# Keeping the traced order on VectorE and ScalarE from the big sets on, and asking sooner for w_down's operands and the last group's weights

## The chip, the cores and the metric

The kernel runs on one core of a Trainium2 chip. The metric is the device time of one execution in microseconds (us), taken as the median of several runs. TensorE is called PE in the profile, VectorE DVE, ScalarE ACT, GpSimd POOL and SyncE SP; SPq, ACTq and POOLq are the DMA queues that these engines issue into.

## The reference, cut to what matters

One transformer block with 512 tokens, width 2048 and a feed-forward width of 5632, all in float32. The mixing half (a latent-attention branch and a gated delta branch) is not touched by the change. What is touched is the second half and the final norm:

```
h = _rmsnorm(x, norm_ffn[l]) * (1.0 + sc_f) + sh_f
gate, up = jnp.split(h @ w_gate_up[l], 2, axis=-1)
x = x + gt_f * ((jax.nn.silu(gate) * up) @ w_down[l])
...
return _rmsnorm(x, final_norm)
```

## The kernel before

**Precision.** Every float32 operand of a matmul is split into two parts: `hi`, a cast on ScalarE to a rounded float32 format, and `lo`, the rest, subtracted on VectorE. A product is then three matmuls: hi with hi, hi with lo, lo with hi. In the trace a weight's halves are `hi` and `lo`, an operand's halves `xh`/`xl` (or `h2h`/`h2l`, `ah`/`al`), and the last group's weights `wl`. `hilo` (lines 238 to 247) makes an operand's two halves: lines 242 (ScalarE) and 243 (VectorE). A weight's halves are made at lines 1718 and 1721 (Strassen sets) or 266 and 267 (plain sets).

**Strassen sets.** `strassen` (line 1673) computes a product of 2 by 2 blocks with seven products, in 16 units. Units 0 to 7 work on four products (`m1`, `m6`, `m7`, `m5`; 24 matmuls a unit), units 8 to 15 on three (`m2`, `m4`, `m3`; 18 matmuls). A unit has a load (`start`, three DMAs of 256 KB on SP's queue), a split (`sums` on VectorE at line 1698, then a cast and a subtraction for each of two weight tiles), its matmuls, and sometimes a step ahead of them (`pre`) or behind them (`post`). In what follows a set's units are called u0 to u15.

**Order of the sets.** B1 to B10 are the big sets, `big(s)`, for w_gate_up (gate and up, then Silu and product in `finish`). Four plain sets dn0 to dn3 (`dn(36, n)`) follow for one group of w_down's rows, then two Strassen sets D0 and D1 (`strassen_down(0, n)`), four more plain sets dn4 to dn7 (`dn(40, n)`), the Strassen sets D2 and D3 (`strassen_down(1, n)`), and the last group (`last_down`): two `last_set`s and eight `token_unit`s, in the trace the matmuls with output `dnt`. A plain set has two units; its four PSUM banks are emptied by four ScalarE activations (tile `y`, line 2066), each followed by an accumulating DMA on POOL's queue. Between the plain sets dn1 and dn2 stand `turned_a` units: four short transposes, whose result is split into `ah` and `al`.

**Operands of the Strassen sets of w_down.** `sums_down(ks)` (line 1952) makes the operands for D0 and D1 (ks=0) or D2 and D3 (ks=1), in four parts q0 to q3; q is used by units 2q, 2q+1 and again 8+2q, 9+2q. A part reads four tiles of 256 KB back from `f_dram` (`a11`, `a21`, `a22`, `a12`, in the trace all named `a`), takes four sums on VectorE (line 1983) and makes seven pairs of halves (lines 242 and 243): 11 operations on VectorE and 7 on ScalarE. `free(q)` says when a part may start, by how many of the earlier operands are `gone`. A part that is not ready when a unit needs it is forced: `ready` (lines 1793 and 1835) steps the generator to the end of that part ahead of the unit's matmuls. While one part is computed, the loads of the next are fetched, one between two steps.

**Chains and the driver.** Generators such as `sums_down` are chains: the driver (line 49) steps each of them once for every 12 matmuls that it emits, and a `yield n` waits n such steps. The driver also loads units ahead: `drv.ahead` says how many units may be loaded beyond the two that are split. It is 4 (`LOADS`), and `pre` of a Strassen set's u0 sets it to 2.

**Order on the engines.** `Ordered` (line 144) wraps an engine: every instruction issued through it keeps its place in the traced order. In the kernel before TensorE, GpSimd and SyncE are wrapped, so the profile gives line 155 for all that they do; VectorE and ScalarE are not, and the scheduler places their instructions as it sees fit, but for those wrapped in `behind` (line 205): the sums of the weights and of the operands on VectorE.

**Last group.** `gated_weights` multiplies the last group's weights with the gate, splits them and writes them to `l_dram` during the big sets. `last_weights(n)` loads eight of these tiles (`wl`, 256 KB each) on SP's queue; n=0, 1, 2 at units 11, 13 and 15 of D3, n=3 ahead of the second `last_set`. `last_rows`, ahead of the first `last_set`, loads four rows of the final norm on the same queue. Each of the eight `token_unit`s (t, n), with n=2 and 3 in turn, is 12 matmuls.

Of the kernel before, what the change touches and what calls it, by code (L numbers as in the profile page):

```python
# [34 lines left out]
class Unit:  # L35


    def __init__(self, load=None, split=None, mms=None, pre=None, post=None, weight=1, alone=False, late=False):
        self.load = load
        self.split = split  # L40
        self.mms = mms
        self.pre = pre
        self.post = post
        self.weight = weight
        self.alone = alone
        self.late = late
# [97 lines left out]
class Ordered:  # L144


    def __init__(self, tc, engine):
        self.tc = tc
        self.engine = engine

    def __getattr__(self, name):
        f = getattr(self.engine, name)

        def call(*args, **kwargs):
            return self.tc.keep_in_program_order(f(*args, **kwargs))  # L155

        return call


class Core:  # L160
    def __init__(self, tc, pinned):
        nc = tc.nc
        for e in ("tensor", "vector", "scalar", "gpsimd", "sync"):
            setattr(self, e, Ordered(tc, getattr(nc, e)) if e in pinned else getattr(nc, e))

# [4 lines left out]
def block_kernel(ctx: ExitStack, tc: tile.TileContext, a: dict, out):  # L172
    nc = Core(tc, PINNED)
    drv = Driver()
# [28 lines left out]
        nc.gpsimd.dma_start(dst, src)  # L203

    def behind(ins):
        return tc.keep_in_program_order(ins)

    mm = nc.tensor.matmul

# [340 lines left out]
    def logits_done(first):  # L550
        def done(ps):
            for j, q in enumerate(ps):
# [6 lines left out]
                        ks=[(k, 1) for k in range(KT)])  # L559
# [900 lines left out]
    def with_pre(units, fn):  # L1460
        u = units[0]
        p0 = u.pre

        def pre():
            fn()
            if p0 is not None:
                p0()
        u.pre = pre
        return units
# [203 lines left out]
    def strassen(w, g, u, par, operand, ready, second_read, finish, freed, extra=None):  # L1673
# [53 lines left out]
        def pre(i):  # L1727
            ready(i % 8 // 2)
            if i == 0:
                drv.ahead = 2  # L1730
                for c, *_ in FIRST4:
                    ps[c] = [PS(c) for _ in range(2)]
            if i == 8 and "act" in chains:
                drv.finish(chains["act"])
# [154 lines left out]
    def gated_weights():  # L1889

        for n in range(4):
            row = gate_row(n)
            for k in range(4):
                w = S("wg")
                side(w[:], w_dn[(LAST + k) * P:(LAST + k + 1) * P, 512 * n:512 * n + 512])
                yield 4
                behind(nc.vector.tensor_tensor(w[:], w[:], row[:], ALU.mult))
                for i, v in enumerate(hilo(w[:], "wg")):
                    side(l_dram[n, k, i], v[:].bitcast(F32))
                w = v = None  # L1900
                yield 4
# [50 lines left out]
    def sums_down(ks):  # L1952

        ahead = []

        def free(q):
            return q < 4 and gone[ks] >= min(q + 2, 4) and (q < 3 or plain_sets[0] > 4 * ks + 3)

        def fetch_a(q):
            v = {}  # L1960
            for name, i, h in (("a11", 8 * ks + q, 0), ("a21", 8 * ks + q, 1), ("a22", 8 * ks + 4 + q, 1), ("a12", 8 * ks + 4 + q, 0)):
                v[name] = S(name)
                load(v[name][:], f_dram[i, h])
                yield 2
            ahead.append(v)

        for q in range(4):
            if not ahead:
                yield from until(lambda: free(q))
                yield from fetch_a(q)  # L1970
                yield 5
            v = ahead.pop(0)
            more = free(q + 1)
            if more:
                fetching = fetch_a(q + 1)
            v["x7"] = S("x7")
            d = {}
            for c, dst, x, y, op in (("m7", "x7", "a11", "a21", ALU.subtract), ("m1", "a11", None, None, None),
                                     ("m5", "a21", "a22", "a21", ALU.subtract), ("m4", "a22", None, None, None),
                                     ("m6", "a11", "a11", "a21", ALU.add), ("m2", "a12", None, None, None),  # L1980
                                     ("m3", "a12", "a11", "a12", ALU.subtract)):
                if op is not None:
                    behind(nc.vector.tensor_tensor(v[dst][:], v[x][:], v[y][:], op))
                d[c] = hilo(v[dst][:], "x")
                if op is None:
                    if more and next(fetching, None) is None:
                        more = False
                    yield
            v = None
            if more:  # L1990
                yield from fetching
            down[ks][q] = d
            made[ks] = q + 1
            yield
# [80 lines left out]
    xc = []  # L2075

    def ffn():
        def gu0():
            us, st = [], {}

            def done(ps):
                done_ = gu_done(0, ps)
                for j in range(4):
                    for h in range(2):
                        done_(j, h)

            for h in range(2):
                half = fm_set("gu0", gu_loads(0), 512, KT, lambda k, h=h: half_k(h2T[h][k // 2], k), done if h else None, st=st,
                              cols=slice(256 * h, 256 * h + 256), alone=True)
                for i, u in enumerate(half):  # L2090
                    def ahead(h=h, k=min(2 * i + 4, KT)):
                        while h2n[h] < k:
                            drv.step(h2c[h])
                    with_pre([u], ahead)
                us.append(half)

            def start():
                for j in range(KT):
                    mixT[j] = None
                start_h2(1)()  # L2100
            with_pre(us[0], start)
            return us[0] + us[1]
# [12 lines left out]
        def last_weights(n):  # L2115

            for k in range(4):
                wl[n, k] = S("wl", F32R), S("wl", F32R)
                for i in range(2):
                    load(wl[n, k][i][:].bitcast(F32), l_dram[n, k, i])  # L2120
# [34 lines left out]
        def last_down():  # L2155
            for i, u in enumerate(strassen_down(1, 1, turned_x2)):
                if 6 <= i < 14:
                    with_pre([u], lambda i=i: x2_back(i - 6))
                if i >= 12:
                    with_pre([u], lambda i=i: reload_a(LAST + i - 12))  # L2160
                if i in (11, 13, 15):
                    with_pre([u], lambda i=i: last_weights((i - 11) // 2))
                yield u
            for n in range(2):
                us = last_set(n)
                if n == 0:
                    with_pre(us, last_rows)
                else:
                    with_pre(us, lambda: last_weights(3))
                yield from us  # L2170
            for t in range(NT):
                for n in (2, 3):
                    yield token_unit(t, n)
# [54 lines left out]
        def scaled(t, y):  # L2228
            for i in range(4):
# [4 lines left out]
                    nc.vector.tensor_scalar(v, v, y[:], None, op0=ALU.mult)  # L2234
                (nc.scalar.dma_start if i % 2 else load)(out[tok(t), 512 * i:512 * i + 512], v)

        yield from gu0()
        yield from with_pre(gu_both(1), lambda: xc.append(drv.add(combine())))
        assert known == {4, 5}
        side(g_dram.rearrange("(k p) -> p k", p=P), gt_ffn[:])  # L2240
        euvw.append(wides.tile([P, 4, 512], F32, tag="wide", name="euvw"))
        drv.add(gated_weights())
        for s in range(1, 11):
            for i, u in enumerate(big(s)):
                if (s, i) == (10, 10):
                    with_pre([u], lambda: maker.__setitem__(0, drv.add(sums_down(0))))
                yield u

# [1 line left out]
            drv.ahead = LOADS  # L2250
        for n in range(4):
            for k, u in enumerate(dn(36, n)):
                yield with_pre([u], more)[0]
                if n in (1, 2):
                    yield Unit(mms=turned_a(2 * n + k - 2), pre=lambda: drv.finish(chains["act"]))
        for n in range(2):
            for i, u in enumerate(strassen_down(0, n)):
                if (n, i) == (1, 10):
                    def start():
                        for k in range(40, 44):  # L2260
                            reload_a(k)
                        maker[1] = drv.add(sums_down(1))
                    with_pre([u], start)
                yield u
        for n in range(4):
            for u in dn(40, n):
                yield with_pre([u], more)[0]
        yield from strassen_down(1, 0)
        yield from last_down()

# [59 lines left out]
```

## Time and profile before

| What | us |
|---|---|
| median of 3 runs | 2822.74 |
| lowest and highest of the runs | 2819.11, 2823.09 |
| the profiled execution | 2822.31 |
| its span, first to last instruction | 2820.5 |
| PE busy in the span | 2737.4 |
| DVE busy | 2012.8 |
| ACT busy | 1136.7 |
| POOL busy | 245.8 |

The profiled execution is 0.43 us under the median; 1.8 us of its time lie outside the span. A times row in the views of the trace starts with a window (from and to, in us from the span's start), its length, and each engine's busy time with the number of its instructions, then the clock granted to TensorE as a share of full speed, the mean share of time in which the 16 DMA engines were busy, and GB/s. A row of a timeline starts with the start and the duration in us; the brackets hold the idle time before the instruction and what ended it. A group's `x4` means four instructions in a row.

### The profile page before, as it was taken

The numbers are of one execution on the slowest core, as the hardware profiler recorded it, in microseconds if no ns is written. First come the engines' busy times: TensorE is split into PE (matmuls) and PEld (weight loads), VectorE is DVE, ScalarE is ACT, GpSimd is POOL, SyncE is SP. The second block draws the span as 40 slices with busy tenths as digits, with TensorE's granted clock in tenths as the row PEclk, the third lists the DMA queues.
The fourth block names the chain that finished last, engine by engine and source line by source line (L and its number), as shares of the span: only waits on it lengthen the run. The fifth ranks groups of instructions, "written<-read, shape, count | busy, mean of one in ns | idle before, by whom it ended". The sixth has DMA issues, their size and how long they took to land. (4 is left out here: it accounts for less than half of the span.)

```text
span 2820.5 us, 37178 instructions
## 1 busy us (share of the span) xinstructions
PE 2737.4 (97%) x13478; PEld 2282.4 (81%) x13478; DVE 2012.8 (71%) x3114; ACT 1136.7 (40%) x1593; POOL 245.8 (9%) x324
## 2 busy tenths in 40 slices
PE   9999999999999999999999999999999997997987
PEld 7888788888888888888997888888888885785775
DVE  8784657676867456883678888777778858767754
ACT  3443333443344332232554444444444444344332
POOL 0000011002100000000001011000000020111033
PEclk9999999999999999999999999999999998998998
DMA  9896556546755468894656667656666686687697
GB/s 353 297 353 203 157 168 185 180 146 184 210 148 179 145 213 277 283 310 138 188 168 211 233 226 239 213 202 199 206 209 214 212 216 187 225 258 182 164 300 214
DMA packets 319969, 606.00 MB, mean 215 GB/s; under 512 B 42948, under 2 KB 79972, under 8 KB 319656
## 3 DMA queue, kind: packets, MB, share of 16 engines
q1 hardware_dynamic: 255544, 482.06, 52.9%
q0 software_dynamic: 27744, 63.23, 8.5%
q10 hardware_dynamic: 36496, 58.34, 5.7%
q8 instruction: 105, 1.72, 0.2%
q14 instruction: 80, 0.66, 0.1%
HBM read 505.97 MB, written 97.53 MB: 214 GB/s over the span
## 5 line engine op out<-in xcount | busy, mean ns | idle before, releaser
L267 DVE TENSOR_TENSOR lo<-raw,hi 128x1024 fp32r<-128x1024 f32 (+1 forms) x274 | 336.8, 1230 | 314.7 <-ACT hi L266 301.0
L266 ACT CAST hi<-raw 128x1024 fp32r<-128x1024 f32 (+1 forms) x274 | 285.1, 1042 | 676.4 <-DMA raw<-in_w_in_dram 133.8
L1718 ACT CAST hi<-raws 128x1024 fp32r<-128x1024 f32 (+1 forms) x336 | 302.1, 908 | 553.7 <-DVE raws L1698 268.0
L1721 DVE TENSOR_TENSOR lo<-raws,hi 128x1024 fp32r<-128x1024 f32 (+1 forms) x336 | 350.4, 1043 | 194.5 <-ACT hi L1718 192.9
L438 DVE CUSTOM_DVE_ANT_0 rawm<-rawm,cbc 128x1024 f32<-128x1024 f32 x192 | 233.8, 1236 | 10.8 <-DMA rawm<-in_w_mod_dram 10.6
L155 PE MATMUL m<-hi,xh 128*128 128x512 f32 x448 | 183.6, 410 | 29.6 <-ACT xh L242 26.8
L155 PE MATMUL m<-lo,xh 128*128 128x512 f32 x448 | 182.2, 407 | 10.1 <-DVE lo L1721 9.9
L155 PE MATMUL m<-hi,h2h 128*128 128x512 f32 x480 | 190.5, 397 | 0.0
L155 PE MATMUL m<-lo,h2h 128*128 128x512 f32 x480 | 187.4, 390 | 1.7 <-DVE lo L1721 1.6
L155 PE MATMUL m<-hi,xl 128*128 128x512 f32 x448 | 182.4, 407 | 5.4 <-DVE xl L243 5.3
L155 PE MATMUL m<-hi,h2l 128*128 128x512 f32 x480 | 187.2, 390 | 0.0
L1698 DVE TENSOR_TENSOR sums<-raws,raws 128x1024 f32<-128x1024 f32 x112 | 136.3, 1218 | 30.2 <-DMA raws<-in_w_down_dram 17.6
L1721 DVE TENSOR_TENSOR lo<-sums,hi 128x1024 fp32r<-128x1024 f32 x112 | 136.3, 1217 | 22.0 <-ACT hi L1718 21.9
L1718 ACT CAST hi<-sums 128x1024 fp32r<-128x1024 f32 x112 | 117.4, 1048 | 51.5 <-PE m L155 51.4
L155 PEld LDWEIGHTS m<-hi,xh 128*128 128x128 f32 x448 | 88.7, 198 | 51.4 <-ACT xh L242 30.2
L155 PEld LDWEIGHTS m<-lo,xh 128*128 128x128 f32 x448 | 88.9, 198 | 32.5 <-DVE lo L1721 13.9
L155 PE MATMUL wo<-mh,hi 128*128 128x512 f32 (+1 forms) x320 | 111.2, 347 | 0.0
L155 PE MATMUL wo<-mh,lo 128*128 128x512 f32 (+1 forms) x320 | 111.0, 347 | 0.0
L155 PE MATMUL wo<-ml,hi 128*128 128x512 f32 (+1 forms) x320 | 110.9, 347 | 0.0
L155 PEld LDWEIGHTS m<-hi,xl 128*128 128x128 f32 x448 | 88.0, 197 | 27.6 <-DVE xl L243 9.6
L155 PEld LDWEIGHTS m<-lo,h2h 128*128 128x128 f32 x480 | 90.3, 188 | 21.2 <-DVE lo L1721 3.6
L155 PEld LDWEIGHTS m<-hi,h2l 128*128 128x128 f32 x480 | 90.1, 188 | 19.2
(521 smaller groups left out, 6896.2 us busy)
## 6 DMA issues: line engine op xcount, KB each, us to landing
raws<-in_w_gate_up_dram SPq DMA_DIRECT2D x400, 256.0 KB, 3.6
rawm<-in_w_mod_dram SPq DMA_DIRECT2D x192, 512.0 KB, 5.5
raw<-in_w_in_dram SPq DMA_DIRECT2D x144, 512.0 KB, 4.6
raws<-in_w_down_dram SPq DMA_DIRECT2D x160, 256.0 KB, 5.1
s_dram<-raws ACTq DMA_DIRECT2D x112, 256.0 KB, 2.2
raws<-s_dram SPq DMA_DIRECT2D x112, 256.0 KB, 3.7
raw<-in_w_o_dram SPq DMA_DIRECT2D x40, 512.0 KB, 4.3
rawa<-in_w_in_dram SPq DMA_DIRECT2D x32, 512.0 KB, 4.1
```

Source lines behind the costliest of these rows:

```text
L155: return self.tc.keep_in_program_order(f(*args, **kwargs))
L266: nc.scalar.copy(hi[:], raw[:])
L267: (lo_eng or nc.vector).tensor_tensor(lo[:], raw[:], hi[:].bitcast(F32), ALU.subtract)
L438: r = nc.vector.tensor_tensor_reduce(raw, raw, c, 1.0, 0.0, ALU.mult, ALU.add, parts[:, k, half:half + 1])
L1698: add = lambda o, x, y: behind(nc.vector.tensor_tensor(o, x, y, ALU.add))
L1718: nc.scalar.copy(hi[:], src)
L1721: nc.vector.tensor_tensor(lo[:], src, hi[:].bitcast(F32), ALU.subtract)
```

## The change

Three things are edited.

**Order.** `Ordered` gets a switch `on`. All five engines are wrapped now, VectorE and ScalarE with the switch off; it is turned on for both just before `gated_weights` is added, which happens while the last units ahead of B1 are fetched. From then on both engines keep the traced order. `behind` does nothing more once the switch is on.

**w_down's operands.** `sums_down(0)` starts at unit 8 of B10 (before: 10), `sums_down(1)` at unit 8 of D1 (before: 10), with the reload of `ah` and `al` for dn4 to dn7 moved from unit 10 to unit 13. `free` lets parts start after 0, 2, 3 and 4 of `gone` (before: 2, 3, 4, 4). `fetch_a` yields once, with no number, after each of its four loads (before: `yield 2`), and `yield 3` (before: 5) follows the fourth. `drv.ahead` is set to 2 at unit 3 of the second plain gate-and-up set and in the last two of each group of four plain sets, no longer in `pre` of a Strassen set.

**Last group's weights.** `last_weights(0..2)` move one unit earlier, to units 10, 12 and 14 of D3; `last_weights(3)` moves from the second `last_set` to the first, ahead of `last_rows`.

```diff
 class Ordered:
-    def __init__(self, tc, engine):
+    def __init__(self, tc, engine, on=True):
...
         def call(*args, **kwargs):
-            return self.tc.keep_in_program_order(f(*args, **kwargs))
+            ins = f(*args, **kwargs)
+            return self.tc.keep_in_program_order(ins) if self.on else ins
...
-            setattr(self, e, Ordered(tc, getattr(nc, e)) if e in pinned else getattr(nc, e))
+            setattr(self, e, Ordered(tc, getattr(nc, e), e in pinned))
...
     def behind(ins):
-        return tc.keep_in_program_order(ins)
+        return ins if nc.vector.on else tc.keep_in_program_order(ins)
...
             if i == 0:
-                drv.ahead = 2
...
         def free(q):
-            return q < 4 and gone[ks] >= min(q + 2, 4) and (q < 3 or plain_sets[0] > 4 * ks + 3)
+            return q < 4 and gone[ks] >= (0, 2, 3, 4)[q] and (q < 3 or plain_sets[0] > 4 * ks + 3)
...
                 load(v[name][:], f_dram[i, h])
-                yield 2
+                yield
             ahead.append(v)
...
                 yield from fetch_a(q)
-                yield 5
+                yield 3
...
-                if i in (11, 13, 15):
-                    with_pre([u], lambda i=i: last_weights((i - 11) // 2))
+                if i in (10, 12, 14):
+                    with_pre([u], lambda i=i: last_weights((i - 10) // 2))
...
                 if n == 0:
-                    with_pre(us, last_rows)
-                else:
-                    with_pre(us, lambda: last_weights(3))
+                    with_pre(us, lambda: (last_weights(3), last_rows()))
...
+        def few():
+            drv.ahead = 2
+
         yield from gu0()
-        yield from with_pre(gu_both(1), lambda: xc.append(drv.add(combine())))
+        us = with_pre(gu_both(1), lambda: xc.append(drv.add(combine())))
+        with_pre([us[3]], few)
+        yield from us
...
+        nc.vector.on = nc.scalar.on = True
         drv.add(gated_weights())
         for s in range(1, 11):
             for i, u in enumerate(big(s)):
-                if (s, i) == (10, 10):
+                if (s, i) == (10, 8):
                     with_pre([u], lambda: maker.__setitem__(0, drv.add(sums_down(0))))
...
-                yield with_pre([u], more)[0]
+                yield with_pre([u], more if n < 2 else few)[0]
...
-                if (n, i) == (1, 10):
+                if (n, i) == (1, 13):
+                    with_pre([u], lambda: [reload_a(k) for k in range(40, 44)])
+                if (n, i) == (1, 8):
                     def start():
-                        for k in range(40, 44):
-                            reload_a(k)
                         maker[1] = drv.add(sums_down(1))
...
-                yield with_pre([u], more)[0]
+                yield with_pre([u], more if n < 2 else few)[0]
```

The loop in `sums_down` that fetches the next part between two steps is unchanged. It reads:

```python
if more and next(fetching, None) is None:
    more = False
```

More of the change, by code (lines that the diff above doesn't have):

```diff
@@ L144 @@
 class Ordered:
-    def __init__(self, tc, engine):
+    def __init__(self, tc, engine, on=True):
         self.tc = tc
         self.engine = engine
+        self.on = on
     def __getattr__(self, name):
```

## The prediction

> **What bounds the kernel now.** First the page: how much of the span TensorE (PE) is busy, and which of its matmuls wait.
>
> ```profile
> span 2820.5 us, 37178 instructions
> ...
> PE 2737.4 (97%) x13478; PEld 2282.4 (81%) x13478; DVE 2012.8 (71%) x3114; ACT 1136.7 (40%) x1593; POOL 245.8 (9%) x324
> ...
> L155 PE MATMUL m<-hi,xh 128*128 128x512 f32 x448 | 183.6, 410 | 29.6 <-ACT xh L242 26.8
> ```
>
> PE is the bound, and no edit takes a matmul away (its instructions and their order are the same in both programs). So only PE's 83 us of idleness, and the slower clock that follows an idle stretch, can be won or added to. The last row says where: matmuls of w_down's Strassen sets wait for the operand's cast. Next, busy time by stage: B2 to dn0, dn0 to dn3, D0, D1, dn4 to dn7, D2, D3.
>
> ```profile
> 1500.00:2300.00 800.00, 798.32 (x3582) 659.22 (x3581) 629.22 (x736) 356.77 (x439) 48.99 (x86) 1.00 0.65 217
> 2279.40:2324.90 45.50, 45.50 (x210) 37.64 (x209) 24.23 (x31) 20.86 (x31) 19.26 (x20) 1.00 0.95 229
> 2324.90:2427.00 102.10, 85.85 (x337) 67.98 (x336) 79.95 (x100) 45.80 (x60) 6.63 (x7) 0.90 0.61 178
> 2427.00:2507.30 80.30, 77.33 (x337) 62.69 (x336) 61.74 (x74) 30.01 (x34) 10.10 (x19) 1.00 0.79 259
> 2507.30:2550.90 43.60, 43.60 (x194) 36.09 (x193) 25.43 (x31) 21.73 (x30) 18.81 (x21) 1.00 1.06 258
> 2550.90:2655.70 104.80, 86.07 (x338) 67.61 (x337) 76.92 (x97) 43.16 (x57) 6.00 (x7) 0.89 0.58 165
> 2655.70:2754.60 98.90, 88.67 (x401) 71.17 (x400) 61.61 (x74) 34.05 (x46) 29.17 (x43) 0.97 0.95 279
> ```
>
> The plain sets and the big sets have no gap worth the name and run at full clock: there is nothing to win there, only something to lose. A Strassen set's 8 x 24 + 8 x 18 = 336 matmuls, 0.227 us apart, need 76.2 us. D0 takes 102.1 and D2 104.8: 25.9 and 28.6 us too many, at a clock of 0.90. D1 is 4.1 over; D3's 98.9 hold 64 short transposes besides. Third, what PE waits for from dn0 on:
>
> ```profile
> PE m L155 <- ACT xh L242: 26.8, 7, 6.6
> PE m L155 <- DVE lo L1721: 9.9, 7, 3.3
> PE dnt L155 <- DMA wl<-l_dram: 6.0, 5, 1.5
> PE m L155 <- DVE xl L243: 5.3, 6, 1.7
> PE m L155 <- ACT y L2066: 2.7, 1, 2.7
> ```
>
> The operand parts (xh, xl) carry 32 of these 51 us. Where they bite, unit by unit (u0, u2, u4, u6 of D0; u1, u2, u4, u6 of D2; ideal 24 x 0.227 = 5.44 us each):
>
> ```profile
> 2324.87:2334.79 9.92, 7.19 (x25) 5.42 (x24) 8.25 (x10) 6.49 (x9) 4.06 (x4) 0.84 0.74 200
> 2340.39:2354.15 13.76, 7.66 (x26) 5.80 (x24) 11.80 (x15) 5.73 (x8) 0.00 (x0) 0.75 0.79 242
> 2359.59:2373.20 13.61, 9.07 (x25) 6.29 (x24) 11.86 (x16) 4.99 (x7) 0.58 (x1) 0.75 0.48 158
> 2378.64:2388.90 10.26, 7.38 (x25) 5.32 (x24) 8.48 (x13) 4.46 (x7) 0.57 (x1) 0.83 0.70 217
> ```
> ```profile
> 2556.29:2568.46 12.17, 5.60 (x25) 4.32 (x23) 7.25 (x9) 4.23 (x6) 0.00 (x0) 0.95 0.86 241
> 2568.46:2582.71 14.25, 9.50 (x24) 6.59 (x25) 12.16 (x16) 4.83 (x7) 0.00 (x0) 0.57 0.37 112
> 2588.15:2601.83 13.68, 9.14 (x26) 6.31 (x24) 11.87 (x16) 4.99 (x7) 0.58 (x1) 0.75 0.51 156
> 2607.27:2617.57 10.30, 7.43 (x25) 5.36 (x24) 8.49 (x13) 4.46 (x7) 0.57 (x1) 0.83 0.69 217
> ```
>
> Over 5.44 they are: D0 4.5, 8.3, 8.2, 4.8; D2 6.7, 8.8, 8.2, 4.9. Part q1 is needed at u2, q2 at u4, q3 at u6. A part of each excess is gap and a part clock (0.57 to 0.95 in these rows).
>
> **The change part by part.** Working base: the profiled execution, 2822.31 us (0.43 under the median), of which 2820.5 are span.
>
> *The end of dn3 and D0's u0.* Operand casts run on ScalarE (ACT) ahead of dn3's evictions, because the part's loads stood on SP behind nine weight loads that took 32.61 us to issue:
>
> ```profile
> 2292.73 32.61 SPq L155 DMA_DIRECT2D raws<-in_w_down_dram  x9
> ```
> ```profile
> 2329.75 2.41 ACT L2066 ACTIVATE y<-dn,gt_ffn 128x512 f32<-128x512 f32 x4
> ```
> ```profile
> 2330.48 0.50 PE L155 MATMUL m<-hi,xh 128*128 128x512 f32 x1 [2.73 <-ACT y L2066]
> ```
>
> The changed program asks for q0 in B10 and q1 from B10's u15 on, with fewer weights loaded ahead: q0 is computed in B10, q1 in dn1 and dn2, and y stands first on ACT. u0's 4.5 and u2's 8.3 us go.
>
> *q2 and q3 of D0.* `fetch_a` now yields None, and the loop takes a None for the end of the fetch. So only `a11` is fetched ahead, then dropped: six loads more (1.5 MB; hidden, DMA share 0.61 in D0), and each part begins its four loads anew once the part before is done. In the traced order q2 falls into D0's u1 to u3 and q3 is still due when u6 needs it, so its whole chain is forced ahead of u6. How long a chain takes is seen in dn2, from the first sum to the last subtraction:
>
> ```profile
> 2304.57 0.68 DVE L1983 TENSOR_TENSOR x<-a,a 128x512 f32<-128x512 f32 x1
> ...
> 2314.40 0.69 DVE L243 TENSOR_TENSOR xl<-a,xh 128x512 fp32r<-128x512 f32 x1 [0.69 <-ACT xh L242]
> ```
>
> That is 10.5 us. In a fixed order it starts after the subtractions of u7's weights, with about 5 us of u5 as cover: a gap of 5.6, and, as the chain alternates between two engines and four sums, three smaller ones (0.3, 2.95, 0.3), with 2 us of clock 11.2 in all, where u6 loses 4.8 now. u4 keeps 0.9 of 8.2. D0: 25.9 to 12.1, **-13.8** (0 if the parts come as late as now, -25.9 if no gap is left).
>
> *D2.* The same, but q2 stands later in the order, in u2 and u3, and its second half behind the subtraction of u5's weights, whose buffers come free only at the end of u3: gap 6.3 and clock 3.4, and u6 7.7 and 2.5. u1's 6.7 and u2's 8.8 go. 28.6 to 19.9, **-8.7** (0 to -28.6).
>
> *The fixed order in the plain sets.* What the scheduler does now between dn1 and dn2: a weight's cast goes ahead of the last eviction.
>
> ```profile
> 2301.76 1.04 ACT L266 CAST hi<-raw 128x1024 fp32r<-128x1024 f32 x1
> 2302.69 0.69 ACT L2066 ACTIVATE y<-dn,gt_ffn 128x512 f32<-128x512 f32 x1
> ```
> ```profile
> 2302.83 1.22 DVE L267 TENSOR_TENSOR lo<-raw,hi 128x1024 fp32r<-128x1024 f32 x1 [4.21 <-ACT hi L266]
> ```
>
> In traced order the cast for the first unit of dn2, and of dn3, stands behind all four evictions, the last of which waits for PE's last matmul. Between lie four transposes, 0.43 us. Cast ready 0.7 + 1.04 + 0.2 = 1.9 us after that matmul, subtraction 3.1: gaps of 1.5 and 0.8, 2.3 a set, **+4.6** for two. dn4 to dn7 have no transposes between them and a unit's cast is emitted a set earlier: nothing. At dn0 the Silus of B10 and q0's rest stand ahead of the weight's halves: cast 1.4 late, subtraction 0.9, a bank 0.9, **+3.2**. At dn4 two banks come from D1's multiplications:
>
> ```profile
> 2505.86 0.69 DVE L1842 TENSOR_TENSOR y<-m,row 128x512 f32<-128x512 f32 x1
> ```
>
> They now stand behind up to ten operations of q0, 0.6 us apart: ready at some 2511.8 where dn4 needs the bank at 2508.7, with the queue behind **+3.8** (0 if the chain is done by then). Clock behind these gaps:
>
> ```profile
> 2331.70:2335.10 3.40, 3.40 (x9) 2.61 (x9) 3.31 (x4) 2.46 (x4) 3.40 (x4) 0.50 0.89 102
> ```
>
> A gap of 2.73 us was followed by 3.4 us at half clock, 1.7 lost. The new gaps, four places, are about that size or under it; I take a little over two such windows, **+4**. New stalls: 15.6 (0 if the queues run ahead of PE by more than the traced order suggests, 26 if each takes two half-clock windows).
>
> The Trainium skill, "TensorE: Matmul & The Clock Gate", Part 1, says the array falls to half clock after an idle window of about 3.4 us; by it the 4 us drop out and the sum would be 2803. The trace does not agree: 2.73 us was enough.
>
> *B1 to B10.* There is one stall:
>
> ```profile
> 1498.22 0.79 PE L155 MATMUL m<-hi,x7h 128*128 128x512 f32 x1 [5.20 <-ACT sl L2012]
> ```
>
> ACT evicts the gate's bank behind casts of the last group's weights and of operands; in traced order fewer of them go first: **-1.5** (0 to -4). In B2 to B10 VectorE is busy 79% and in traced order sums stand ahead of subtractions as before: 0.
>
> *D3 and the last group.* D3's DMA share is 0.95; unit 14's weights now queue behind eight wl loads: **+1** (-3 to +4). Then wl: the last eight stand behind the norm's rows.
>
> ```profile
> 2755.29 6.04 SPq L155 DMA_DIRECT2D norm<-in_final_norm_dram  x4
> 2762.95 14.50 SPq L155 DMA_DIRECT2D wl<-l_dram  x8
> ```
> ```profile
> 2776.47:2797.45 20.98, 14.94 (x50) 10.24 (x49) 10.17 (x20) 3.82 (x12) 8.21 (x7) 0.76 0.63 152
> ```
>
> These 48 matmuls need 10.9 us and take 21.0; wl lands one by one, 14.5 / 8 = 1.8 us apart. Issued 7.7 us earlier, the last is there when its matmul is due, but for 2 us: **-8** (0 to -10.1). The rows of the norm come later, and nothing of PE needs them.
>
> Sum: -13.8 - 8.7 + 4.6 + 3.2 + 3.8 + 4 - 1.5 + 1 - 8 = -15.4. **2807 us.**
>
> **The rivals.** *A, slower: the fixed order hands the operands' DMA waits to everything behind.* A sum that waits for a late `a12` now stops VectorE, and with it the weights' halves that the scheduler would have taken first. It decides if a part's last load lands more than the 5 us of one unit after its turn, as it would if SP is blocked again as in the 32.61 us row. Then D0 and D2 keep their excess, and -22.5 drops out of the sum: +7.1, 2829. For it: q3 and D2's q2 are loaded late. Against: DMA share 0.6 in D0 and D2. The Trainium skill, same page, "Engine queue depths", has ScalarE and VectorE as strict FIFOs; the 32.61 us row shows SP held in that way, and no row of before shows VectorE so.
>
> *B, better: the gaps in the plain sets and at dn4 don't appear*, because the casts need only 1.9 us after a matmul and the first product's banks absorb it: -15.6 more, 2791. Against: dn units have no slack in matmuls between sets.
>
> *C, the weights asked for sooner come no sooner*: in the last stretch the DMA engines are the bound (0.95 in D3), so order on SP moves nothing: 2815.
>
> **How the numbers follow.** Forecast (2797 to 2817) 0.45, A 0.24, B 0.19, C 0.12. The range 2788 to 2832 holds forecast, B, C and most of A. About 0.2%, 5.6 us, is what a measurement of this kernel can tell from no change. Faster by more: nearly all of the forecast and B, over half of C, 0.66; within: the rest of C and a little of forecast and A, 0.12; slower 0.22.
>
> **What would show it.** After should have no gap at D0's u0 and u2 and D2's u1 and u2; gaps behind ACT xh ahead of u6 in D0 and D2, 5 to 8 us, and at D2's u4; new gaps of 1 to 3 us at dn0, dn2, dn3, dn4; six more loads from f_dram; and, in the last group, waits for wl under 2 us. I am wrong if D0 and D2 stay above 100 us, or if B2 to B10 lose time, since nothing above gives the big sets a gap.

## The result, and the profile after

The changed kernel takes 2830.62 us (median of 5 runs, 2827.70 to 2832.08) against 2821.77 for the kernel before in the same comparison (5 runs, 2817.19 to 2823.09): a ratio of 1.0034, 95% interval 1.0020 to 1.0049. It is slower by some 9 us where 15 us less were forecast. The time lies in the stated range, the sign is the wrong one.

The page of the changed kernel (all engines now go through the helper at line 156):

```profile
span 2830.2 us, 37160 instructions
...
PE 2739.6 (97%) x13478; PEld 2283.4 (81%) x13478; DVE 2021.4 (71%) x3114; ACT 1138.1 (40%) x1593; POOL 245.8 (9%) x324
...
L156 PE MATMUL m<-hi,xh 128*128 128x512 f32 x448 | 182.9, 408 | 22.1 <-ACT xh L156 22.1
L156 PE MATMUL m<-lo,xh 128*128 128x512 f32 x448 | 182.9, 408 | 19.1 <-DVE lo L156 19.1
```

The waits for the operand's cast fell, from 26.8 to 22.1 us. In their place stands the wait for the weight's second half, `lo`: 25.0 us, where it was 11.5 before. What PE waited for, from the list of its waits:

```profile
PE m L156 <- DVE lo L156: 25.0, 12, 6.3
PE m L156 <- ACT xh L156: 22.1, 6, 6.7
...
PE dn L156 <- ACT hi L156: 5.7, 3, 3.1
...
PE dn L156 <- DVE y L156: 3.8, 1, 3.8
```

The stages, by busy time, cut at their first matmuls: B2 to B9, dn0 to dn3, D0, D1, dn4 to dn7, D2, D3, the last group, the tail behind the last matmul.

```profile
1570.25:2202.57 632.32, 628.33 (x2817) 516.14 (x2816) 503.76 (x585) 281.68 (x347) 36.19 (x67) 1.00 0.65 215
...
2282.40:2339.85 57.45, 51.63 (x209) 40.40 (x210) 32.39 (x41) 26.99 (x40) 20.14 (x22) 0.91 0.85 198
2339.85:2433.27 93.42, 83.09 (x338) 66.61 (x337) 68.81 (x83) 39.96 (x51) 5.23 (x6) 0.91 0.61 185
2433.27:2516.97 83.70, 78.27 (x338) 64.06 (x337) 62.98 (x77) 30.77 (x36) 9.68 (x18) 0.98 0.77 249
2516.97:2566.19 49.22, 45.43 (x193) 37.11 (x192) 31.66 (x41) 24.03 (x34) 19.71 (x22) 0.97 0.84 198
2566.19:2669.07 102.88, 84.94 (x338) 67.56 (x337) 70.31 (x84) 40.24 (x51) 5.17 (x6) 0.88 0.64 191
2669.07:2769.37 100.30, 88.41 (x402) 71.75 (x400) 62.38 (x75) 34.76 (x46) 30.14 (x44) 0.95 0.97 291
2769.37:2812.77 43.40, 43.40 (x194) 35.96 (x193) 23.07 (x49) 12.63 (x32) 22.31 (x22) 1.00 0.81 193
2812.77:2830.20 17.43, 0.39 (x2) 0.00 (x0) 8.92 (x33) 8.73 (x16) 0.00 (x0) 0.61 0.50 185
```

Two rows of the kernel before that the prediction does not show, B2 to B9 and the tail:

```profile
1574.04:2201.35 627.31, 625.73 (x2818) 516.79 (x2816) 499.55 (x585) 281.88 (x347) 36.19 (x67) 1.00 0.65 216
2808.10:2820.50 12.40, 0.39 (x2) 0.00 (x0) 5.12 (x21) 4.50 (x8) 0.00 (x0) 0.70 0.50 188
```

D0 won 8.7 us and the last group 10.1, as the lengths say; D2 won only 2.0. The plain sets lost 12.0 and 5.7, B2 to B9 5.0, D1 3.4, and the tail, which the prediction left out, 5.0.

How each loss looks. In the big sets PE waits mostly for the first `lo` of a set's second unit. Two things now stand ahead of that subtraction on VectorE. In B2 a subtraction `wgl` of the last group's weights waits 0.69 us for its cast, and in the fixed order everything behind it on VectorE waits too; PE then stands 1.73 us (0.56 before). Before, another operation was put into that hole and `wgl` had no wait. First row: VectorE after; second: VectorE before; third: PE after.

```profile
1573.12 0.69 DVE L156 TENSOR_TENSOR wgl<-wg,wgh 128x512 fp32r<-128x512 f32 x1 [0.69 <-ACT wgh L156]
```
```profile
1577.42 0.68 DVE L243 TENSOR_TENSOR wgl<-wg,wgh 128x512 fp32r<-128x512 f32 x1
```
```profile
1578.06 0.50 PE L156 MATMUL m<-lo,h2h 128*128 128x512 f32 x1 [1.73 <-DVE lo L156]
```

The other is the second sum of the next unit, `raws<-sums,raws`. The traced order has it ahead of the subtraction `lo<-raws`; the scheduler had put the subtraction first. VectorE after, then before:

```profile
1576.18 0.69 DVE L156 TENSOR_TENSOR raws<-sums,raws 128x512 f32<-128x512 f32 x1
1576.79 1.22 DVE L156 TENSOR_TENSOR lo<-raws,hi 128x1024 fp32r<-128x1024 f32 x1
```
```profile
1579.16 1.21 DVE L1721 TENSOR_TENSOR lo<-raws,hi 128x1024 fp32r<-128x1024 f32 x1
1580.30 0.68 DVE L1698 TENSOR_TENSOR raws<-sums,raws 128x512 f32<-128x512 f32 x1
```

From B5 on this alone is left: the last `wgl` is computed at 1774.21, in B4, and B5 to B9 lose 0.3 us each all the same. In B6 the subtraction starts 4.56 us behind the set's first matmul, before the change 3.91.

At dn2 the cast stands behind the four evictions, as forecast (ScalarE, then PE, both after):

```profile
2307.68 2.41 ACT L156 ACTIVATE y<-dn,gt_ffn 128x512 f32<-128x512 f32 x4
2309.97 1.06 ACT L156 CAST hi<-raw 128x1024 fp32r<-128x1024 f32 x1
```
```profile
2311.08 0.50 PE L156 MATMUL dn<-ah,hi 128*128 128x512 f32 x1 [3.10 <-ACT hi L156]
```

In D1 and D3 VectorE stands for a late load, and the subtraction behind it stands too. In D1 the sum for u7 waits 6.83 us for its weights (8.28 in D3), u6's `lo<-raws` comes behind it, and PE waits 4.23 us for that (6.33 in D3). Before, the subtraction went ahead of the sum. VectorE in D1 after, then before:

```profile
2468.88 1.22 DVE L156 TENSOR_TENSOR sums<-raws,raws 128x1024 f32<-128x1024 f32 x1 [6.83 <-DMA raws<-in_w_down_dram]
...
2470.74 1.22 DVE L156 TENSOR_TENSOR lo<-raws,hi 128x1024 fp32r<-128x1024 f32 x1
```
```profile
2457.80 1.23 DVE L1721 TENSOR_TENSOR lo<-raws,hi 128x1024 fp32r<-128x1024 f32 x1 [1.25 <-ACT hi L1718]
2463.85 1.22 DVE L1698 TENSOR_TENSOR sums<-raws,raws 128x1024 f32<-128x1024 f32 x1 [4.83 <-DMA raws<-in_w_down_dram]
```

In D2 the weight buffers come free late. On ScalarE the cast of dn7's last weights stands behind operand casts of q1 and four evictions, 8.8 us ahead of D2's first matmul (21.7 us ahead in the kernel without the fixed order, below). SP issues three of the six loads in its row at once and the other three, u1's, only some 20 us later, when the subtraction behind that cast has freed a buffer. u2's loads follow and land late; VectorE's sum waits 5.59 us for them; PE stands 4.03 us at u2, where the prediction had no gap. ScalarE, SP, VectorE and PE after:

```profile
2557.39 1.06 ACT L156 CAST hi<-raw 128x1024 fp32r<-128x1024 f32 x1
```
```profile
2538.84 22.26 SPq L156 DMA_DIRECT2D raws<-in_w_down_dram  x6
```
```profile
2579.92 1.23 DVE L156 TENSOR_TENSOR sums<-raws,raws 128x1024 f32<-128x1024 f32 x1 [5.59 <-DMA raws<-in_w_down_dram]
```
```profile
2583.06 0.80 PE L156 MATMUL m<-lo,xh 128*128 128x512 f32 x1 [4.03 <-DVE lo L156]
```

### The profile page after: what moved, and what is told of

The parts are those of the page before. It is cut to its first block, busy times and chain, and to the rows that moved or that the text cites. A ratio compares the mean times of both kernels' runs of the same rounds, so it can differ in the third digit from the quotient of the medians.

```text
span 2830.2 us, 37160 instructions
## 1 busy us (share of the span) xinstructions
PE 2739.6 (97%) x13478; PEld 2283.4 (81%) x13478; DVE 2021.4 (71%) x3114; ACT 1138.1 (40%) x1593; POOL 245.8 (9%) x324
## 5 line engine op out<-in xcount | busy, mean ns | idle before, releaser
L156 PE MATMUL m<-hi,xh 128*128 128x512 f32 x448 | 182.9, 408 | 22.1 <-ACT xh L156 22.1
L156 PE MATMUL m<-lo,xh 128*128 128x512 f32 x448 | 182.9, 408 | 19.1 <-DVE lo L156 19.1
```

The lines of the kernel that those rows point to most:

```text
L156: ins = f(*args, **kwargs)
```

## The experiments

The first theory after the result: asking sooner is what wins, the fixed order on VectorE and ScalarE is what loses, in small pieces everywhere. Its rival: the requests themselves, in front of the weights' loads on SP, cost what they win, and the order only hands that on. The part ahead of B1 took between 1486.3 and 1491.8 us in the profiles, and both ends are from kernels without an edit there (weights only, weights and rows); so stages are compared by their lengths, and totals by medians and ratios to the kernel before.

There are two limits. A profile is one execution: those of sooner only, fetch goes on and all three are 5.4, 5.4 and 6.5 us under the median of their kernel, and D0 takes 88.67 us in sooner and fetch and 84.56 in all three, whose programs are the same up to there. And the kernel before has its own median in each comparison (2821.43 for the first four experiments of the table, 2823.88 for the next four, 2824.33 for the last four), so kernels of different comparisons are compared by their ratios.

| Kernel | median, us | ratio to before, 95% |
|---|---|---|
| changed kernel | 2830.62 | 1.0034 (1.0020 to 1.0049) |
| order in big sets | 2825.64 | 1.0016 (1.0007 to 1.0024) |
| sooner only | 2805.48 | 0.9947 (0.9936 to 0.9959) |
| weights only | 2819.35 | 0.9990 (0.9981 to 0.9999) |
| fetch goes on | 2819.56 | 0.9994 (0.9985 to 1.0003) |
| sooner and fetch | 2788.00 | 0.9873 (0.9860 to 0.9887) |
| weights and rows | 2815.65 | 0.9972 (0.9962 to 0.9982) |
| parts later | 2780.02 | 0.9847 (0.9833 to 0.9860) |
| all three | 2782.81 | 0.9854 (0.9838 to 0.9869) |
| order on ScalarE | 2822.15 | 0.9986 (0.9977 to 0.9995) |
| order on VectorE | 2828.49 | 1.0011 (1.0002 to 1.0020) |
| later and rows | 2772.84 | 0.9817 (0.9803 to 0.9831) |
| norm on VectorE | 2771.61 | 0.9807 (0.9794 to 0.9821) |

### Order in big sets

To the kernel before, with the switch in `Ordered` and `few` at unit 3 as in the change:

```diff
+        nc.vector.on = nc.scalar.on = True
         drv.add(gated_weights())
...
+                if (s, i) == (10, 8):
+                    nc.vector.on = nc.scalar.on = False
```

> The kernel before, with VectorE and ScalarE in traced order only from the start of B1 to unit 8 of B10, and two units loaded ahead in the last units ahead of B1 as in the changed kernel; everything behind is as before. Theory 1 (the fixed order itself costs, in small pieces in every stage): the start and B1 win some 4 us, B2 to B9 lose some 5 (B2 +1.7, B3 +0.7, B4 +1.1, B5 to B9 +0.3 each), the rest is unchanged: 2820 to 2825. Rival (B2 to B10 lose because w_down's parts and the loads are asked for sooner): B2 to B9 as long as before, 78.1 us from B5 on, and with the gain in B1 2817 to 2819.

Measured: 2825.64, 4 us above the kernel before, just over the first theory's range. B2 to B9 from the busy times:

```profile
1570.23:2202.69 632.46, 628.49 (x2817) 515.99 (x2816) 503.82 (x585) 282.05 (x347) 36.31 (x67) 1.00 0.64 215
```

They lose 5.2 us, set by set within 0.2 us of what the changed kernel loses (1.7, 0.7, 1.3, then 0.3 each), with none of w_down's parts asked for sooner. The loss of the big sets is the order's.

### Sooner only

The changed kernel without the line that turns the switch on:

```diff
-        nc.vector.on = nc.scalar.on = True
```

> The changed kernel with the switch for VectorE and ScalarE never turned on: all that is asked for sooner stays, the scheduler orders the two engines again. Theory 1 (the gains come from asking sooner, the losses from the fixed order): big sets, plain sets and dn4 as in the kernel before, D0 and D2 each at least 9 and 2 us shorter than before, the last group 10 shorter, its tail as before (12.4 us): 2790 to 2802. Rival (the loads asked for sooner stand in front of the weights' loads on SP, and the fixed order only hands on what they hold up): D1 and D3 keep their 3 us each, D2's u2 its gap behind the weights' load, dn4 its 3.8: 2812 to 2830.

Measured: 2805.48, slightly over the first theory's range and 25.1 us (2830.62 - 2805.48) below the changed kernel, 24.5 by the ratios. B2 to B9, dn0 to dn3, D2:

```profile
1563.85:2191.18 627.33, 625.70 (x2817) 516.67 (x2816) 499.68 (x585) 282.35 (x347) 36.30 (x67) 1.00 0.65 216
2269.26:2320.90 51.64, 47.35 (x210) 38.69 (x208) 33.38 (x43) 27.30 (x41) 20.16 (x22) 0.97 0.87 209
...
2544.81:2640.11 95.30, 82.08 (x338) 65.59 (x337) 68.38 (x84) 39.49 (x50) 6.06 (x7) 0.91 0.61 183
```

The big sets are as before, D2 is 7.6 us shorter than with the order (102.88 - 95.30), dn1 to dn3 are as before, D1 and D3 within 0.7 us of it. But dn0 and dn4 keep 6 us each: these two belong to asking sooner, as the rival has it. And the tail is 16.0 us, not the 12.4 of the first theory. B1 is 7.0 us shorter than before, its stall gone, without any order; the earlier `drv.ahead` = 2 is this kernel's only edit ahead of it. With the order on top B1 takes 4.5 us more (81.43 against 76.94).

### Weights only

To the kernel before, the move of `last_weights` alone:

```diff
-                if i in (11, 13, 15):
-                    with_pre([u], lambda i=i: last_weights((i - 11) // 2))
+                if i in (10, 12, 14):
+                    with_pre([u], lambda i=i: last_weights((i - 10) // 2))
...
-                    with_pre(us, last_rows)
-                else:
-                    with_pre(us, lambda: last_weights(3))
+                    with_pre(us, lambda: (last_weights(3), last_rows()))
```

> The kernel before with the move of the last group's weights alone. Both theories expect the third group of 48 matmuls of the last group to fall from 21.0 to 10.9 us. Theory 1 (in the changed kernel the 5 us of longer tail come from the fixed order on VectorE, where each sum waits for the square ahead of it): the tail stays near 12.4 us, time 2810 to 2814. Rival (the tail grows because the rows of the final norm land 8 us later and PE no longer gives VectorE time to catch up): the tail is 15 to 18 us, time 2815 to 2819.

Measured: 2819.35, 2 us below before. The last group is 9.9 us shorter, the tail 8.8 longer: the first theory was wrong here, the rival right on the cause, though the tail is longer than its 15 to 18 us and the time a little over its range. The tail, and VectorE's first multiplication with a row of the norm:

```profile
2796.79:2818.00 21.21, 0.39 (x2) 0.00 (x0) 11.67 (x47) 10.66 (x22) 0.00 (x0) 0.58 0.52 198
```
```profile
2786.25 1.59 DVE L2216 TENSOR_TENSOR x2t<-x2t,norm 128x512 f32<-128x512 f32 x1 [7.57 <-DMA norm<-in_final_norm_dram]
```

VectorE stands 7.57 us for the rows that now land behind the weights.

### Fetch goes on

The changed kernel, one word changed:

```diff
                 load(v[name][:], f_dram[i, h])
-                yield
+                yield 1
```

> The changed kernel, its bare yield in the fetch of a part made a yield 1, so that the loop doesn't take it for the end: all four loads of the next part are fetched ahead, and six loads fewer are made. Theory 1 (D0 and D2 kept most of their excess because parts q2 and q3 were fetched anew and forced): q2 is made in the plain sets, D0's u4 falls from 12.8 to under 7 us, D2's u2 and u4 from 12.1 and 14.4 to under 8; D0 and D2 6 to 10 us shorter each: 2811 to 2819. Rival (VectorE is full in D0 and D2, 12 to 14 us of work between u3 and u6, and a part that is made sooner only moves the gap): D0 and D2 within 3 us of the changed kernel: 2826 to 2834.

Measured: 2819.56, 11.1 us below the changed kernel, just over the first theory's range. Loads of `a` from f_dram are 32 again, where the changed kernel makes 38. dn0 to dn3, D0, D2:

```profile
2281.25:2342.65 61.40, 50.94 (x209) 39.40 (x209) 37.98 (x50) 30.64 (x47) 20.14 (x22) 0.94 0.73 160
2342.65:2429.07 86.42, 80.03 (x337) 64.53 (x336) 63.30 (x73) 36.33 (x44) 5.24 (x6) 0.94 0.67 201
2567.80:2654.72 86.92, 79.17 (x338) 63.74 (x337) 63.13 (x73) 36.18 (x44) 5.17 (x6) 0.96 0.69 209
```

D0 is 7.0 and D2 16.0 us shorter than in the changed kernel; each group of four plain sets, where q2 is made now in fixed order, takes 4 more, and D1 1.6. D0's u4 is down to 5.44 us. The lost fetch is a cause of its own.

### Sooner and fetch

The edits of sooner only and of fetch goes on together.

> All that is asked for sooner, no fixed order on VectorE and ScalarE, and the fetch that goes on (yield 1). Theory 1 (the two losses, order and broken fetch, are separate and add): against the kernel without fixed order (2805.5) D0's and D2's u4 lose 7 to 8 us each more, q2's work in the plain sets finds free time, since the scheduler lets the weights' casts pass it: 2788 to 2798. Rival (q2's chain in the plain sets costs there what it saves in D0 and D2, with or without the fixed order): dn0 to dn3 9 us longer than without it, 2802 to 2810.

Measured: 2788.00, the low end of the first theory's range. D0 and D2:

```profile
2325.15:2413.82 88.67, 82.05 (x337) 65.87 (x336) 62.64 (x75) 35.08 (x43) 5.82 (x7) 0.94 0.70 210
2544.13:2626.31 82.18, 78.94 (x337) 63.93 (x336) 61.45 (x73) 35.31 (x43) 6.10 (x7) 0.98 0.71 207
```

D2 is 6 us from its 76.2, and its u4 lost the 8 us that were expected (13.63 to 5.44); D0's lost only 3.1 (12.69 to 9.55). Without the fixed order q2's work in the plain sets costs 1.4 us (dn2).

### Weights and rows

To weights only, the four rows of the norm at unit 10 of D2 (the loop that loads them stands in `norm_rows` now, no longer in `last_rows`):

```diff
+        us = strassen_down(1, 0)
+        with_pre([us[10]], norm_rows)
+        yield from us
```

> The kernel before, the last group's weights asked for sooner, and the four rows of the final norm loaded at unit 10 of D2 instead of ahead of the first set of the last group. Theory 2 (the weights' gain of 10 us is given back because the rows land 8 us later and VectorE's multiplications with them start late): the tail falls from 21.2 to 12 to 15 us, 2810 to 2814. Rival (the tail is bound by the sums, squares and multiplications themselves once PE doesn't wait): tail 18 us or more, 2816 to 2821.

Measured: 2815.65, between the two; the tail is 15.8 us. The rows account for 5.4 of the tail's 8.8 us. What stays goes with VectorE's multiplications by rows (minimum, median, maximum in ns), here and in the kernel before:

```profile
L2218 DVE TENSOR_TENSOR x2t<-x2t,norm x8: 686/691/4593, 2781.3 to 2804.9; 128x512 f32<-128x512 f32 x8
```
```profile
L2218 DVE TENSOR_TENSOR x2t<-x2t,norm x8: 683/691/4368, 2780.9 to 2811.3; 128x512 f32<-128x512 f32 x8
```

One of the eight takes 4593 ns where the median takes 691. The kernel before has it too, 4368 ns, but there PE stood for `wl` in the same stretch, so VectorE had time to catch up. The last experiment tests this.

### Parts later

To sooner and fetch, the parts started at unit 10 of B10 and of D1 again:

```diff
-                if (s, i) == (10, 8):
+                if (s, i) == (10, 10):
...
-                if (n, i) == (1, 8):
+                if (n, i) == (1, 10):
```

> The same as sooner and fetch, with the start of the parts put back to unit 10 of B10 and of D1. Theory 3 (dn0's and dn4's 6 us come from q0, asked for two units sooner, whose work stands ahead of the plain sets' halves and of the multiplications that empty dn4's banks): dn0 and dn4 10.9 us each again, D0 and D2 unchanged: 8 to 12 us below sooner and fetch. Rival (the chain only moves: it then stands in dn0 and dn1, dn4 and dn5, and holds their halves): within 4 us of it.

Measured: 2780.02, 8.0 us below, as theory 3 has it but for dn0, which stays 1.9 us above the kernel before. dn4 is at 11.15 us (10.88 before, 15.87 in sooner and fetch), dn0 at 12.79 (15.95):

```profile
2487.15:2498.30 11.15, 11.15 (x49) 8.93 (x48) 11.15 (x20) 4.81 (x7) 2.60 (x5) 1.00 0.72 252
```

D0 is as it was, D2 2.6 longer. So q0, asked for two units sooner, stood in the way of the operations that empty the banks for dn0 and dn4: in sooner and fetch PE waits 3.14 us there for ScalarE's `g` and 3.10 us for VectorE's `y`, here 1.61 us and not at all.

### All three

Sooner and fetch with the rows in D2.

> Sooner and fetch, and the rows of the norm at unit 10 of D2. Theory 2: the tail falls from some 16 to 12 us, 3 to 5 us below sooner and fetch, 2784 to 2795. Rival: tail 15 us or more, no difference of over 2 us.

Measured: 2782.81, 5.2 us below sooner and fetch and a little under the range of theory 2; its four runs lie between 2776.35 and 2789.14, so the 5.2 are not sharp. The tail falls from 20.8 to 16.0, not to 12: there the rival was right.

### Order on ScalarE, order on VectorE

The changed kernel with the switch on for one engine:

```diff
-        nc.vector.on = nc.scalar.on = True
+        nc.scalar.on = True
```

> The changed kernel with the fixed order turned on for ScalarE alone; VectorE is scheduled as before. Theory 1a (each stage's loss belongs to one engine; the casts behind the evictions in dn2 and dn3 are ScalarE's, all else VectorE's): dn0 to dn3 as in the changed kernel, 57 us together, B2 to B9 and D2 as with no fixed order: 2808 to 2814. Rival (the two hand their waits to each other, and either order alone costs most of the 25 us): 2822 to 2832.

and the same with `nc.vector.on = True` alone:

> The changed kernel with the fixed order turned on for VectorE alone. Theory 1a: B2 to B10 lose 5 to 7 us, D1, D2 and D3 3, 7 and 1, dn2 and dn3 nothing: 2818 to 2826. Rival: 2822 to 2832 with gaps at dn2 and dn3 as well, or, if only both together cost, 2803 to 2810.

Measured: 2822.15 and 2828.49. ScalarE alone, dn0 to dn3 and D2; VectorE alone, B2 to B9:

```profile
2273.96:2331.17 57.21, 51.61 (x209) 40.49 (x209) 32.48 (x41) 26.99 (x40) 20.15 (x22) 0.91 0.86 197
2554.44:2656.76 102.32, 83.50 (x338) 66.06 (x337) 71.27 (x87) 40.27 (x51) 6.06 (x7) 0.92 0.65 191
```
```profile
1571.32:2204.90 633.58, 628.97 (x2818) 515.84 (x2816) 504.05 (x585) 281.58 (x347) 36.32 (x67) 1.00 0.64 214
```

Both times are over the ranges of theory 1a and within those of the rival. The plain sets go by ScalarE, the big sets by VectorE, as theory 1a has it, and D1 by VectorE: its u6 takes 13.1 us with VectorE's order, 9.3 with ScalarE's (11.5 with both, 9.5 with neither). But D2 loses its 7 us by ScalarE's order alone. There, as in the changed kernel, SP issues u1's loads 6.45 us ahead of D2's first matmul, in sooner only 19.3 us ahead.

By the ratios ScalarE's order costs some 11 us over sooner only, VectorE's some 18, both together 25: less than the sum. So neither theory holds whole. Most stages go by one engine, but in B1 and D2 either order costs (2.7 and 6.0, 7.0 and 3.6 us), and both together no more than 4.5 and 7.6. The tails (19.1 and 18.6 us against 16.0 in sooner only) show nothing about the order: with ScalarE's, the first multiplication waits 9.5 us for the rows of the norm, and it waits 8.7 in sooner and fetch, which has no order and a tail of 20.8.

### Later and rows, norm on VectorE

Parts later with the rows in D2:

> Parts later (sooner and fetch, the parts started at unit 10 again) with the rows of the norm loaded in D2. Theory 2: the tail falls from 21.5 to 16 us, 2773 to 2777. Rival: what the rows win is lost elsewhere, 2778 to 2782.

and that, with

```diff
-            (nc.gpsimd if n < 2 else nc.vector).tensor_tensor(x_[:], x_[:], norms[n][:], ALU.mult)
+            nc.vector.tensor_tensor(x_[:], x_[:], norms[n][:], ALU.mult)
```

> The same as later and rows, with the multiplications by the norm's rows for the first two sets on VectorE instead of GpSimd. Theory 5 (with the rows there in time, what keeps the tail at 16 us is VectorE's first multiplication, which takes 4.6 to 5.1 us instead of 0.69 while GpSimd's run): that multiplication takes 0.7 us, the tail 12 to 13 us, 2768 to 2773. Rival (eight multiplications more on VectorE, 5 us, and the tail is bound there): 2774 to 2780.

Measured: 2772.84, a hair under the range of theory 2, and 2771.61, the tails 15.6 and 12.2 us. With all sixteen multiplications on VectorE none is long:

```profile
L156 DVE TENSOR_TENSOR x2t<-x2t,norm x16: 682/687/693, 2726.4 to 2761.9; 128x512 f32<-128x512 f32 x16
```

Theory 5 is right on the tail; between the two kernels 1.2 us remain, within their spread (2771.84 to 2775.56 and 2767.61 to 2773.30). Both beat the kernel before by 1.8 to 1.9%.

## Why the prediction was wrong

| Step | forecast, us | measured, us |
|---|---|---|
| B1 | -1.5 | -2.5 |
| B2 to B10 | 0 | +6.8 |
| dn0 to dn3 | +7.8 and clock | +12.0 |
| D0 | -13.8 | -8.7 |
| D1 | 0 | +3.4 |
| dn4 | +3.8 and clock | +5.7 |
| D2 | -8.7 | -2.0 |
| D3 | +1 | +1.4 |
| last group | -8 | -10.1 |
| tail | 0 | +5.0 |

With 1.3 us less ahead of B1 the right column gives the +9.7 of the two spans. The gap of 1.28 us ahead of dn0's first matmul is counted in B10. The largest misses are B2 to B10 (6.8), D2 (6.7), D0 (5.1), the tail (5.0) and D1 (3.4).

The working that failed first is the one that priced the fixed order: it was charged only to the plain sets (15.6 with its clock), while its whole price, by sooner only, is some 25 us, and the 7.0 for dn0 and dn4 among the 15.6 are not the order's, since sooner only keeps them. B2 to B10 losing time is a sign of being wrong that the prediction itself named; of the other, D0 and D2 above 100 us, half came true (93.4 and 102.9).

- **"In B2 to B10 ... in traced order sums stand ahead of subtractions as before: 0."** Not as before: the scheduler had put the first subtraction ahead of the next unit's second sum, and the traced order puts it some 0.6 us later. And a third kind of instruction was not looked at: the last group's weights have a cast between two of their VectorE operations, and in the changed kernel each of these pairs leaves VectorE idle for some 0.7 us, up to B4. Order in big sets shows the 5.2 us by itself, order on VectorE alone 6.3, order on ScalarE alone 0.4.
- **D1 at 0.** VectorE's wait for u7's load holds u6's subtraction. This needs VectorE's order, as the two runs with one engine's order show (u6 13.1 against 9.3 us).
- **"28.6 to 19.9" for D2.** u1's and u2's 15.5 us were to go. The operands were there in time, but u1 and u2 then waited for their weights, 5.2 + 2.2 us won. The step that failed is the "nothing" for dn4 to dn7: dn5 to dn7 are indeed as long as before, but the cast held back in dn7 holds the buffer that D2's loads need. In sooner only u1 and u2 take 5.44 us each; order on ScalarE alone brings 4.5 us back there.
- **"u4 keeps 0.9 of 8.2" for D0.** It kept 7.4, and keeps it without the fixed order as well. Here the lost fetch was seen, but priced only at u6: q2, too, begins its loads anew, and its chain ends after u4 is due. Fetch goes on removes all of u4's excess (8.2 us against before).
- **"Nothing of PE needs them"** of the norm's rows. True, and beside the point: the kernel ends 12.4 us behind PE's last matmul, with work of VectorE and ScalarE. A window for the tail was never quoted, and no term stood for it. In the changed kernel no multiplication waits for the rows; but PE no longer stands for `wl` while VectorE is at its long multiplication. Kernels with the rows in time and no fixed order have tails of 15.6 to 16.0 us, and 12.2 where that multiplication is gone; what makes it 17.4 here was not taken apart. Weights only shows a second way to lose what PE won: 9.9 us, 8.8 of them given back, 5.4 by the late rows.
- **Right:** u0 and u2 of D0 (-4.5 and -8.3, exactly the excess named); the cast behind the evictions at dn2 and dn3 (gaps of 3.4 and 1.8 us, 2.3 forecast for each); the forced q3, about 5 us dearer than before; the last group's weights, about 2 us off.
- **Near by luck:** dn4's bank, 3.79 us where 3.8 was forecast, since its cause is the earlier q0, not the order (sooner only keeps it). B1, -2.5 where -1.5 was forecast from the order: sooner only wins 7.0 there, and the order takes 4.5 of it back. D3, +1.4 where +1 was forecast for weights queued behind `wl`: weights only has that queue, and its D3 is 0.6 us shorter than before.

Rival A gave the time, 2829, and the family of the cause: a wait handed on in a fixed order. That the time fits is luck, for its place was wrong. D0 did not keep its excess, and the loads that were waited for were the weights', not a part's. Where a sum does stop VectorE and with it a weight's half is u6 of D1 and D3. And the kernel before did have a row of that kind: its sum at 2463.85, shown above, stood 4.83 us for a load, with a subtraction behind it for which PE then waited 2.47 us. Rival B was excluded by the gaps at the plain sets; C was wrong on the wait for wl, which went, and near the truth on what it is worth, because of the tail.

The rule that small gaps don't slow the clock, weighed in the prediction, would have been wrong here too. At dn0 gaps of 1.28 and 0.53 us were followed by 3.4 us at half clock (PE, then the busy times of that stretch):

```profile
2282.40 0.50 PE L156 MATMUL dn<-ah,hi 128*128 128x512 f32 x1 [1.28 <-ACT hi L156]
...
2283.66 0.50 PE L156 MATMUL dn<-ah,lo 128*128 128x512 f32 x1 [0.53 <-DVE lo L156]
```
```profile
2284.10:2287.50 3.40, 3.34 (x9) 2.13 (x8) 2.71 (x6) 3.26 (x5) 0.00 (x0) 0.51 0.73 222
```

What stays open: how the earlier `drv.ahead` = 2 removes B1's stall, and why the changed kernel's tail is longer still than 16 us.

## What to carry to other kernels

A fixed order costs where it puts an operation that waits (a sum for its load, a subtraction for its cast) ahead of one that the busiest engine needs next, and the scheduler had put the other one first. Look for such pairs over the whole stretch in which the order holds, also in stages without gaps, and ask whose buffers a late operation holds: the price can fall due in the next stage. When a transfer is asked for sooner, look at what it is put in front of, and at the engine that ends the kernel: a stall of the busiest engine can be the time in which the last one catches up. A look-ahead that breaks off quietly shows in the count of loads (38 for 32), so count them.

## What was not expected of the hardware

VectorE's multiplication of two SBUF operands took 4.96 us once in the changed kernel, 4.59 in weights and rows, 4.37 in the kernel before, instead of 0.69, each time while GpSimd's multiplications ran:

```profile
2795.64 4.96 DVE L156 TENSOR_TENSOR x2t<-x2t,norm 128x512 f32<-128x512 f32 x1 [0.79 <-ACT sq L156]
```

The Trainium skill, "SBUF — State Buffer", section "Who interferes with whom", says that a VectorE instruction with two SBUF inputs contends with a GpSimd instruction that reads SBUF, and calls the pair of ports that they share an exclusive lock. The runs agree: with GpSimd's multiplications moved to VectorE all sixteen took 0.68 to 0.69 us, and the tail lost 3.4 us (15.6 to 12.2). Why the longest takes only 1.6 us in weights only, sooner only and sooner and fetch, where the rows land late, is open.
